# Neighbourhood scores of two heads side by side in TensorE, bias tables staged early, and an odd layer's weights loaded into the block spilled first

## The chip, the cores and the metric

The kernel runs as one program on the eight NeuronCores of one Trainium2 chip, two dies of four cores (cores 0 to 3 and 4 to 7). Each core serves 512 context tokens (two prompts) and 1024 latent tokens (one sample). The metric is the device time of the slowest core in microseconds (us).

A program on all eight cores has a slow state, in which one die runs at a lower granted TensorE clock; runs in that state are left out of every ratio. Besides it there is a milder disturbance that still counts as fast: some or all cores of one die run at a mean granted clock of about 0.98 instead of about 0.99, and the time is some 15 us longer. Beside the ratios I use a second number, the **undisturbed die**: of every run, slow ones too, each die on which no core's mean clock is below 0.986 gives the span of its slowest core, and I take the median over these dies. The cut at 0.986 is my choice.

## The reference, cut to what matters

Four layers share one residual stream y. Even layers join a short gated convolution with attention of eight heads of 64 channels; odd layers join pooling with latent attention, whose keys and values are expanded from a compressed form by `w_kv_b`. Every layer has a modulated norm and a squared-ReLU MLP.

```python
def modulate(x, g, shift, scale):
    return rms_norm(x, g) * (1 + scale) + shift

def na_latent(q, k, v, k_ctx, v_ctx, rpb):        # even layers, latent tokens, 64 columns x 16 rows
    ...                                           # keys: 8 neighbouring rows x 16 columns, and 256 cached ones
    s_loc = einsum('brcqhd,brkcjhd->bhrcqkj', qg, kb) * scale
    s_loc = s_loc + bias                          # bias = rpb[head, row offset, column offset]
    s_loc = where(valid, s_loc, NEG_INF)
    s_ctx = einsum('brcqhd,bmhd->bhrcqm', qg, k_ctx) * scale
    p = softmax(concatenate([s_loc, s_ctx], -1))
    ...

def mla_kv(ckv, kpe, w_kv_b, gk):                 # odd layers
    kv = ckv @ w_kv_b                             # the expansion
    ...
```

Of the kernel before, what the change touches and what calls it, by code (L numbers as in the profile page):

```python
# [6 lines left out]
F32 = mybir.dt.float32  # L7
BF16 = mybir.dt.bfloat16
# [83 lines left out]
class Prog:  # L92
# [103 lines left out]
    def schedule(self):  # L196
# [47 lines left out]
        while ndone < total:  # L244
            pick = None
            for e in self.ENG:
# [22 lines left out]
                if pick is None or tmin < pick[0]:  # L269
                    pick = (tmin, e, items)  # L270
            if pick is None:
                self.stuck(cand, ndone)
            tmin, e, items = pick
# [214 lines left out]
def build(depth=4):  # L488
# [43 lines left out]
    with ExitStack() as st:  # L532
# [195 lines left out]

        def SQUARE(out, in_, reads, writes, key=None):

            P.add(("act", "dve"), {"act": [act_fn(out, in_, AF.Square, None, None)],
                                   "dve": [lambda h: h.tensor_tensor(out=R(out), in0=R(in_), in1=R(in_), op=ALU.mult)]}, reads, writes,
                  {"act": act_dur(out, None, None), "dve": vdur(fsize(out))}, key=key)
# [114 lines left out]
        def norm(l, which, tb, key=None):  # L848
# [15 lines left out]
            for kc in range(8):  # L864
                tm, btm = ntr.next()
                STT(tm[:], yT[:, tb, kc, :], Asc[:, l, kc, m:m + 1], r, ALU.mult, ALU.mult,
                    [by[tb][kc], bmw, br], [btm], key=key)
# [4 lines left out]
                SHIFT(o, i_, mod[:, l, sh0 + kc, m:m + 1], ALU.add, [btm, bmw], [bh[tb][kc]], key=key)  # L872
# [109 lines left out]
        def even_bufs(tbs, ar):  # L982
# [4 lines left out]
            e.qTm, b = ar.take((128, 8, n), BF16, 8 * nb, "q")  # L987
            e.bq = {tb: [b[h * nb + k] for h in range(8)] for k, tb in enumerate(tbs)}
# [14 lines left out]
        def even_fixed(e):  # L1003

            MEMSET(e.Vx[:, :, :, 64:128], 1.0, [e.bones])
            qv = e.qTm.rearrange("p (j two) t -> p j two t", two=2)
            for tb in e.tbs:
                MEMSET(qv[64:128, :, 0, lo(tb)], 0.0, e.bq[tb])
                MEMSET(qv[0:64, :, 1, lo(tb)], 0.0, e.bq[tb])
# [30 lines left out]
        def qk_tile(l, e, which, tb, j, w, bw):  # L1040
# [11 lines left out]
            if which == 0:  # L1052
                for a in range(2):
                    ps_ = slice(a * 64, a * 64 + 64)
                    STT(e.qTm[ps_, 2 * j + a, lo(tb)], pt[ps_, :], gqna_sb[ps_, i:i + 1], r[ps_, :], ALU.mult, ALU.mult,
                        [pt.b, br, bsm], [e.bq[tb][2 * j + a]])
# [46 lines left out]
        def attT(e):  # L1103
            return e.qTm.rearrange("p (j two) t -> p two j t", two=2)[:, 0]

        def batt(e):
            return {tb: [e.bq[tb][2 * j] for j in range(4)] for tb in e.tbs}
# [9 lines left out]

        def even_att_p(l, e, key, zones):
            for j in range(4):
                P.key = key + j * 0.01  # L1120
                for a in range(2):
                    h = 2 * j + a
                    s_ = PT(P, 2, zone=zones[0])
                    MMG([(s_[:, (s * 2 + c) * 256:(s * 2 + c + 1) * 256], e.kT[:, j, s * 256 + c * 128:s * 256 + (c + 1) * 128],
                          e.qTm[:, h, s * 256:(s + 1) * 256], True, True) for s in range(2) for c in range(2)],
                        [e.bk[0][j], e.bq[0][h]], [s_.b])
                    p_, bp = e.Pr.next()
                    ACT(p_[:], s_[:], AF.Exp, [s_.b], [bp])
                    acc = PT(P, 1, zone=zones[1])
                    MMG([(acc[:, s * 256:(s + 1) * 256], vo(e, s * 2 + c, h), p_[:, (s * 2 + c) * 256:(s * 2 + c + 1) * 256], c == 0, c == 1)  # L1130
                         for s in range(2) for c in range(2)], [bp, e.bones] + e.bV[0:4], [acc.b])
                    head_out(e, h, acc, 0)

        def even_att_s(l, e, key):
            i = l // 2
            kof = lambda c, b: (c // 2) * 512 + b * 256 + (c % 2) * 128
            RG = [(0, 8, 0, 4), (0, 12, 0, 0), (4, 16, 1, 0), (8, 16, 1, 0)]
            for j in range(4):
                for a in range(2):
                    h = 2 * j + a  # L1140
                    hk = key + h * 0.1
                    P.key = hk
                    tt_, btt = e.Tt.next()
                    for u in range(4):
                        sg, bsg = e.stg.next()
                        DMA("sp", [(sg[:], rpbx[i][h * 4 + u])], [], [bsg], "stg%d" % u, key=hk - 0.3)
                        ACT(tt_[:, u // 2, (u % 2) * 480:(u % 2) * 480 + 480], sg[:], AF.Exp, [bsg], [btt[u]], key=hk - 0.1)
                    acc = [PT(P, 1, zone=[4]), PT(P, 1, zone=[5])]
                    work = [("c", 0), ("c", 1), ("r", 1), ("r", 0), ("r", 2), ("r", 3)]
                    for n, (kind, c) in enumerate(work):  # L1150
                        P.key = hk + (n - 2) * 0.01
                        s_ = PT(P, 2, zone=[0, 2])
                        sv = s_[:].rearrange("p (b x) -> p b x", b=2)
                        p_, bp = e.Pr.next()
                        if kind == "c":
                            MMG([(sv[:, b, :], e.kcT[:, j, c * 128:(c + 1) * 128], e.qTm[:, h, b * 512:512 + b * 512], True, True)
                                 for b in range(2)], [e.bkc, e.bq[1][h], e.bq[2][h]], [s_.b])
                            ACT(p_[:], s_[:], AF.Exp, [s_.b], [bp])
                            its = [(acc[b][:], vo(e, 8 + c, h), p_[:, b * 512:(b + 1) * 512], c == 0, False, True) for b in range(2)]
                            MMG(its[0:1], [bp, e.bones, e.bV[8 + c]], [acc[0].b], key=hk + n * 0.01)  # L1160
                            MMG(its[1:2], [bp, e.bones, e.bV[8 + c]], [acc[1].b], key=hk + n * 0.01)
                            continue
                        r0, r1, u, i0 = RG[c]
                        nr = r1 - r0
                        qs = e.qTm[:, h, :].rearrange("p (r x) -> p r x", x=64)
# [732 lines left out]
```

## The kernel before: the parts that the change touches

A helper records every operation; a list scheduler then puts each engine's operations in order by estimated start times and a priority `key`. Channels lie in the 128 partitions, so two heads of 64 channels share a tile. In the kernel before, q of each head was stored in its own full-height tile whose other 64 rows are zero, so that a full 128-row matmul against the keys of both heads gives one head's scores:

```python
e.qTm, b = ar.take((128, 8, n), BF16, 8 * nb, "q")
...
MEMSET(qv[64:128, :, 0, lo(tb)], 0.0, e.bq[tb])      # the other head's rows
MEMSET(qv[0:64, :, 1, lo(tb)], 0.0, e.bq[tb])
```

The bias enters as a product: exp(s + bias) = exp(s) · exp(bias). A head has four tables of 128x480 values (`rpbx`), loaded as f32 into four stage buffers `stg`, sent through an exp into `Tt`, and multiplied in:

```python
for a in range(2):                                   # one head after the other
    h = 2 * j + a
    for u in range(4):
        sg, bsg = e.stg.next()
        DMA("sp", [(sg[:], rpbx[i][h * 4 + u])], [], [bsg], "stg%d" % u, key=hk - 0.3)
        ACT(tt_[:, u // 2, (u % 2) * 480:(u % 2) * 480 + 480], sg[:], AF.Exp, [bsg], [btt[u]], key=hk - 0.1)
    ...
    MMG([(sv[:, b, 0:nr * 40]..., e.kT[:, j, kof(c, b):kof(c, b) + 128],
          qs[:, r0:r1, b * 24:b * 24 + 40], True, True) for b in range(2)], ...)   # scores, 128 rows
    ACT(pv, sv[:, :, 0:nr * 40], AF.Exp, [s_.b], [bp])
    TT(pv, pv, tv, ALU.mult, [bp] + btt[2 * u:2 * u + 2], [bp])                    # times the table
    ...                                                                          # times V, full height
```

`stg` and `Tt` share the memory of the context group's keys and values, so in layer 0 no table can be asked for before the context attention is done.

In the odd layers the second and third block of y are saved to HBM ("spilled") and their memory is used for weights. `w_kv_b` went where the block that is spilled last had been:

```python
ya, yb = spill(l, 1), spill(l, 2)
o = odd_s_bufs(ya, yb)
...
US = Slot(ya)
```

The norm was one multiply by two factors on DVE and then a shift on ACT or DVE:

```python
STT(tm[:], yT[:, tb, kc, :], Asc[:, l, kc, m:m + 1], r, ALU.mult, ALU.mult, ...)   # y * A * rstd
SHIFT(o, i_, mod[:, l, sh0 + kc, m:m + 1], ALU.add, ...)
```

The softmax here doesn't subtract the row's maximum and nothing guards it: scores larger than these inputs give would overflow.

## Time and profile before

| | before |
|---|---|
| median of 3 runs | 2410.29 us (2410.05 to 2416.41) |
| profiled run | 2394.7 us, spans of the cores 2379.0 to 2392.3 us, clocks 0.991 to 0.996 |
| TensorE (PE) busy, slowest core | 2289.2 us, 96% |

The profiled run was a quick one. The page of the slowest core starts with the engines' busy time, its share of the span and the number of instructions; its part 4 gives the engines' shares of the chain of waits that ended last:

```profile
...
PE 2289.2 (96%) x14455; PEld 1133.0 (47%) x14455; DVE 1068.7 (45%) x1668; ACT 1193.6 (50%) x1845; POOL 227.7 (10%) x377
...
PE 85%; ACT 5%; DMA 4%; DVE 3%; issue 3%; POOL 0%; DVEq 0%; ACTq 0%; POOLq 0%; SPq 0%
...
```

TensorE is the limit: nearly all of the time is its work, and the question is always where it works less or starves less. The next fence is from the groups of instructions by shape, core 0: line, engine, operation, what it reads and writes, shape, count, then busy us and mean ns of one. A busy time that sums overlapping pipelined matmuls is not the time that they take: a stream of 128x512 matmuls advances one per 0.216 us, though each lasts 0.38.

```profile
...
L644 PE MATMUL psall<-arena 128*128 128x512 bf16 x672 | 155.5, 380 | 2.3 <-DVE arena L694 1.0 <-ACT nrstd L668 0.8 <-ACT arena L668 0.5
...
L1796 PE MATMUL psall<-ones 128*128 128x128 bf16 x693 | 47.2, 229 | 0.7 <-issue 0.7
...
L644 PE MATMUL psall<-arena 128*128 128x320 bf16 x192 | 38.1, 299 | 2.4 <-ACT arena L668 1.3 <-DVE arena L679 0.7
...
L644 PE MATMUL psall<-arena 128*128 128x480 bf16 x64 | 18.2, 366 | 0.2 <-ACT arena L668 0.2
...
L644 PE MATMUL psall<-arena 128*128 128x256 bf16 x128 | 17.6, 274 | 0.0
...
```

All shapes have 128 rows: scores and products with V can't be told apart by shape, and no matmul of 64 rows exists. The 693 matmuls on `ones` are fillers that the scheduler puts into gaps to keep the clock up.

Layer 0's attention, by stretches of core 0: start and end, length, busy time of each engine, then PEclk (the granted TensorE clock), the DMA engines' busy share, and GB/s.

```profile
...
120.00:140.00 20.00, 20.00 (x97) 9.25 (x95) 10.96 (x18) 12.69 (x21) 0.02 (x1) 1.00 0.13 27
140.00:160.00 20.00, 20.00 (x160) 10.70 (x159) 11.91 (x21) 13.57 (x23) 1.57 (x3) 1.00 0.58 106
...
180.00:190.00 10.00, 9.16 (x74) 4.49 (x72) 4.77 (x10) 3.08 (x6) 1.06 (x2) 1.00 1.01 173
190.00:200.00 10.00, 10.00 (x120) 6.11 (x118) 6.92 (x12) 5.82 (x9) 1.10 (x3) 1.00 1.00 179
200.00:210.00 10.00, 5.53 (x28) 2.44 (x25) 1.18 (x2) 1.29 (x3) 0.48 (x1) 1.00 1.02 208
210.00:220.00 10.00, 6.93 (x26) 2.99 (x27) 7.19 (x11) 4.39 (x8) 0.00 (x0) 0.66 1.04 201
...
```

From 200 to 220 us TensorE works 12.5 of 20 us while DMA is full; from 120 to 140, DMA is nearly idle. The timeline of ACT in the same place (start, length, instruction; in brackets the idle time before it and what ended it) shows the exps of the tables, 128x480:

```profile
...
182.55 1.58 ACT L668 ACTIVATE arena<-arena 128x480 bf16<-128x480 f32 x3
...
189.59 0.60 ACT L668 ACTIVATE arena<-arena 128x480 bf16<-128x480 f32 x1 [2.27 <-DMA arena<-rpbx]
...
198.95 0.60 ACT L668 ACTIVATE arena<-arena 128x480 bf16<-128x480 f32 x1
...
204.22 0.60 ACT L668 ACTIVATE arena<-arena 128x480 bf16<-128x480 f32 x1 [3.71 <-DMA arena<-rpbx]
209.82 0.60 ACT L668 ACTIVATE arena<-arena 128x480 bf16<-128x480 f32 x1 [5.00 <-DMA arena<-rpbx]
...
```

They come as their loads land. The chain of waits in this place, in order of time, is one such load (start, us, what):

```profile
...
184.42 25.32 DMA arena<-rpbx
...
```

In the odd layer, all four loads of `w_kv_b` are issued late, after POOL's queue waited 6.7 us for a norm (the view of one tile, core 0):

```profile
...
L742 POOL DMA_DIRECT2D yT<-w_kv_b x4: 873/877/955, 728.1 to 730.8; - x4
...
  DVE hT L723: 6.7, 1
...
```

### The profile page before, as it was taken

How to read it: one execution, taken by the hardware profiler on the slowest of the kernel's cores; microseconds unless marked ns; L12 is line 12 of the kernel's file. 1: busy time of each engine (PE TensorE's matmuls, PEld its weight loads, DVE VectorE, ACT ScalarE, POOL GpSimd, SP SyncE). 2: the span in 40 equal slices, each digit the busy share in tenths (PEclk: the TensorE clock that was granted, in tenths of full speed). 3: DMA queues.
4: the chain of work that ended last, by engine and by line, in shares of the span. 5: the costliest groups of instructions: out<-in, count | busy, mean ns of one | idle time of the engine just before them, and what ended most of it. 6: DMA issues, size and time to landing. Idle time of an engine off the chain costs nothing.

```text
span 2392.3 us, 38889 instructions; the slowest of 8 cores (2379.0 to 2392.3 us)
## 1 busy us (share of the span) xinstructions
PE 2289.2 (96%) x14455; PEld 1133.0 (47%) x14455; DVE 1068.7 (45%) x1668; ACT 1193.6 (50%) x1845; POOL 227.7 (10%) x377
## 2 busy tenths in 40 slices
PE   5998999999999999999999999999999999899999
PEld 4454444444444555444444444444445445444444
DVE  2555654324546643323444666531454674243222
ACT  2763636133546675622643775515334657662233
POOL 3100000010001300000002001000100120000000
PEclk9999999999999999999999999999999999999999
DMA  9759686579365778523666666765955635322342
GB/s 184 148 85 177 164 149 129 106 135 153 76 169 78 137 162 142 102 45 83 127 145 146 133 151 131 146 124 114 158 106 133 115 78 120 69 53 53 73 86 88
DMA packets 75286, 285.61 MB, mean 119 GB/s; under 512 B 28896, under 2 KB 41952, under 8 KB 47328
## 3 DMA queue, kind: packets, MB, share of 16 engines
q0 software_dynamic: 52240, 205.27, 50.5%
q1 hardware_dynamic: 22864, 77.87, 9.6%
q8 instruction: 119, 1.95, 0.3%
q14 instruction: 63, 0.52, 0.1%
HBM read 456.23 MB, written 30.54 MB: 203 GB/s over the span
## 4 chain that ended last, share of the span: by engine, by line
PE 85%; ACT 5%; DMA 4%; DVE 3%; issue 3%; POOL 0%; DVEq 0%; ACTq 0%; POOLq 0%; SPq 0%
PE psall L644 84%; ACT arena L668 3%; DMA arena<-rpbx 2%; DVE arena L679 1%; DMA WT<-ada_w 1%; PE psall L652 1%; DVE arena L694 1%; DVE ntmp L694 1%; DMA arena<-mlp_w 1%; PE psall L1796 1%; DMA WT<-mlp_w 0%; ACT psall L668 0%; ACT hT L668 0%; DMA yT<-even_conv 0%; POOL rtmp L679 0%
## 5 line engine op out<-in xcount | busy, mean ns | idle before, releaser
L694 DVE SCALAR_TENSOR_TENSOR yT<-psall,mod,yT 128x512 f32<-128x512 f32 x480 | 358.9, 750 | 680.5 <-PE psall L644 679.9
L644 PE MATMUL psall<-arena,WT 128*128 128x512 bf16 x2688 | 594.9, 379 | 2.6 <-DVE rtmp L679 1.4
L644 PE MATMUL psall<-hT,arena 128*128 128x512 bf16 x2472 | 551.3, 379 | 2.6 <-DVE hT L716 1.5
L668 ACT ACTIVATE arena<-psall 128x512 bf16<-128x512 f32 (+6 forms) x629 | 408.7, 660 | 215.1 <-PE psall L644 171.9
L644 PEld LDWEIGHTS psall<-arena,WT 128*128 128x128 bf16 x2688 | 260.4, 98 | 310.3 <-issue 4.0
L668 ACT ACTIVATE psall<-psall 128x512 f32<-128x512 f32 (+1 forms) x330 | 191.7, 581 | 413.8 <-PE psall L644 412.7
L644 PE MATMUL psall<-arena 128*128 128x65 bf16 (+9 forms) x2960 | 368.1, 273 | 22.9 <-ACT arena L668 15.1
L644 PEld LDWEIGHTS psall<-hT,arena 128*128 128x128 bf16 x2472 | 240.2, 98 | 287.8 <-issue 3.4
L644 PE MATMUL psall<-hT,WT 128*128 128x512 bf16 x1504 | 345.3, 381 | 8.8 <-ACT hT L668 3.5
L644 PEld LDWEIGHTS psall<-arena 128*128 128x128 bf16 (+1 forms) x2960 | 196.6, 97 | 185.0 <-issue 42.7
L668 ACT ACTIVATE nsq<-yT 128x1024 bf16<-128x1024 f32 x66 | 69.6, 1055 | 338.7 <-PE psall L644 211.9
L644 PEld LDWEIGHTS psall<-hT,WT 128*128 128x128 bf16 x1504 | 144.9, 98 | 179.2 <-issue 19.4
L668 ACT ACTIVATE arena<-psall,rk 128x1024 bf16<-128x1024 f32 (+1 forms) x224 | 196.6, 933 | 60.7 <-PE psall L644 56.2
L644 PE MATMUL psall<-hT,yT 128*128 128x512 bf16 x704 | 166.1, 381 | 11.9 <-ACT arena L668 10.3
L694 DVE SCALAR_TENSOR_TENSOR ntmp<-yT,A,nrstd 128x512 f32<-128x512 f32 x192 | 136.3, 750 | 45.4 <-ACT nrstd L668 41.0
L668 ACT ACTIVATE hT<-ntmp,mod 128x512 bf16<-128x512 f32 x161 | 111.3, 719 | 29.0 <-DVE ntmp L694 28.1
L644 PEld LDWEIGHTS psall<-hT,yT 128*128 128x128 bf16 x704 | 68.5, 98 | 92.5 <-issue 15.9
L694 DVE SCALAR_TENSOR_TENSOR arena<-psall,cst_sb,rstd 64x512 bf16<-64x512 f32 (+2 forms) x102 | 76.2, 748 | 75.4 <-ACT rstd L668 72.9
L742 POOL DMA_DIRECT2D WT<-mlp_w x56 | 30.3, 542 | 611.0 <-PE psall L644 608.0
L644 PE MATMUL psall<-arena,yT 128*128 128x512 bf16 (+3 forms) x480 | 77.5, 304 | 1.6 <-ACT arena L668 0.8
L679 DVE TENSOR_TENSOR mod<-psall,cst_sb 128x8 f32<-128x8 f32 x48 | 7.9, 165 | 157.5 <-PE psall L644 157.0
L668 ACT ACTIVATE psall<-psall,eps_sb 128x512 f32<-128x512 f32 x84 | 55.3, 658 | 33.3 <-PE psall L644 33.1
(111 smaller groups left out, 1466.3 us busy)
## 6 DMA issues: line engine op xcount, KB each, us to landing
WT<-mlp_w POOLq DMA_DIRECT2D x56, 1024.0 KB, 9.9
arena<-ada_w POOLq DMA_DIRECT2D x38, 1024.0 KB, 11.2
arena<-mlp_w POOLq DMA_DIRECT2D x32, 1024.0 KB, 9.8
ysc<-yT SPq DMA_DIRECT2D x9, 2048.0 KB, 8.0
yT<-ysc SPq DMA_DIRECT2D x18, 1024.0 KB, 13.2
arena<-rpbx SPq DMA_DIRECT2D x64, 240.0 KB, 7.6
yT<-even_conv POOLq DMA_DIRECT2D x12, 768.0 KB, 9.6
WT<-ada_w POOLq DMA_DIRECT2D x8, 1024.0 KB, 10.8
```

Of the source, the lines that this page charges most:

```text
L644: h.matmul(R(out), lhsT=lhsT, rhs=rhs, start=start, stop=stop, skip_group_check=skip))
L652: fns = [lambda h, o=o, a=a: h.transpose(R(o), a, ident[:, :]) for (o, a) in items]
L668: return lambda h: h.activation(out=R(out), in_=R(in_), func=func, **kw)
L679: fn = [lambda h: h.tensor_tensor(out=R(out), in0=R(in0), in1=R(in1), op=op)]
L694: P.add("dve", [lambda h: h.scalar_tensor_tensor(out=R(out), in0=R(in0), scalar=scalar, in1=R(in1), op0=op0, op1=op1)], reads, writes, vdu ...
L742: fns = [lambda h, o=o, i_=i_: h.dma_start(out=o, in_=i_) for (o, i_) in pairs]
L1796: P.warm = lambda h, o: h.matmul(o, lhsT=ones[:, :], rhs=ones[:, :], start=True, stop=True)
```

## The change

Its intent, in the order of expected worth:

1. q of two heads in one tile (half the memory, no zeros). Scores of the two heads as two 64-row matmuls that can run at once in the upper and lower half of TensorE. Attention goes by pairs of heads and half images.
2. The smaller q leaves room for the four stage buffers elsewhere, so that the first four tables are asked for earlier. The next pair's tables go through the same four buffers.
3. `w_kv_b` and the weights of the query expansion (`w_q_b`) go into the block of y that is spilled first; the pooling projection's weights and output, which had been there, go into the other one. And the first block's projections go ahead of the cache's expansion.
4. The norm becomes a plain multiply, on DVE or POOL, whichever the scheduler finds free, and a scale-and-shift on ACT or DVE. The scheduler breaks ties by priority.

The core of the diff, with cuts marked:

```diff
-            e.qTm, b = ar.take((128, 8, n), BF16, 8 * nb, "q")
+            e.qT, b = ar.take((128, 4, n), BF16, 4 * nb, "q")
...
+        def scores(tile, pairs, reads, key=None):
+            for (out, lhsT, rhs) in pairs:
+                for a in range(2):
+                    r = slice(a * 64, a * 64 + 64)
+                    fns.append(lambda h, o=out(a), l=lhsT(r), x=rhs(r): h.matmul(R(o), lhsT=l, rhs=x, start=True, stop=True))
...
             for j in range(4):
+                t2, btt = e.Tt.next()
                 for a in range(2):
                     for u in range(4):
                         sg, bsg = e.stg.next()
-                        DMA("sp", [(sg[:], rpbx[i][h * 4 + u])], [], [bsg], "stg%d" % u, key=hk - 0.3)
+                        DMA("sp", [(sg[:], rpbx[i][(2 * j + a) * 4 + u])], list(after), [bsg], "stg%d" % u, key=hk - 0.3)
...
-            e.stg = ring(ar, (128, 480), F32, 4, "stg")
+            e.stg = ring(Arena(e.stg_off), (128, 480), F32, 4, "stg")
...
-                STT(tm[:], yT[:, tb, kc, :], Asc[:, l, kc, m:m + 1], r, ALU.mult, ALU.mult, ...)
+                TT(tm[:], yT[:, tb, kc, :], r, ALU.mult, [by[tb][kc], br], [btm], eng="any", key=key)
...
-                SHIFT(o, i_, mod[:, l, sh0 + kc, m:m + 1], ALU.add, ...)
+                SCALE(o, i_, Asc[:, l, kc, m:m + 1], mod[:, l, sh0 + kc, m:m + 1], ...)
...
-            o = odd_s_bufs(ya, yb)
+            o = odd_s_bufs(yb, ya)
...
-            US = Slot(ya)
+            US = Slot(yb)
-            P.key = T + 4
-            kv_block(l, o, "c", ck, bck)
             for tb in (1, 2):
                 odd_prod(l, o, tb, T + 1 + (tb - 1) * 4)
+                if tb == 1:
+                    P.key = T + 4
+                    kv_block(l, o, "c", ck, bck)
```

## The prediction

> **What bounds the kernel.** The page shows PE busy 2289 of 2392 us (96%); the chain of waits is 84% PE matmuls, with pieces of ACT (3%) and of loads of `rpbx` (2%). A stream of 128x512 matmuls advances one per 0.216 us (eight in 1.89 us, the last being 0.38 long). Time is thus PE work plus places where PE starves: about 103 us idle and about 39 us of warm-up matmuls on `ones` (693, each about 0.056 us).
>
> **Scores by two heads.** Per even layer, scores stream 64 heads-by-keys matmuls of about 512 to 256 columns. Summed over both even layers from the groups by shape (64x512, 64x320, 64x480 and 64x256 columns at 0.42 ns each): about 42 us. As two 64-row halves side by side, ideally 21 us. The Trainium skill, "TensorEngine Tiling (Array Packing)", Key Properties, says that changing the tiling mode drains TensorE. No 64-row matmul exists in the trace before, so I cannot measure that. There are 64 score groups per even layer, nearly all between full-height matmuls, so about 256 mode changes. A matmul's latency beyond its stream time is 0.16 us (0.38 - 0.22), an upper estimate of a drain; then 41 us would be lost, twice the gain. I take about 0.05 us: 13 us back. Net 8 us saved, possibly 20, possibly a small loss. AV matmuls and exp elements stay equal; exps per pair of heads go from 12 to 14 (about 0.2 us each, ACT is 70 to 80% busy there, not limiting).
>
> **Layer 0 tables.** The timeline shows p attention holding the buffers for bias tables until 174 us; `rpbx` loads then start behind saturated DMA, ACT waits 7.0 and 6.6 us, and PE sits idle 10.3 us at 189 to 199 (busy 8.9 of 20). Half-size q frees room, so four loads come early. I expect 8 to 10 us saved, some given back because total bytes stay the same and DMA is about 75% busy until 340 us. The second table wait (269 us, PE about 4 us idle) may stay.
>
> **Odd layers.** `w_kv_b` is loaded at 735 us, only after the norm of the third block freed its y (POOL waits 6.9 us for hT); from 721 to 736 PE has only norm sums, warm-up matmuls (about 70) and 4 us idle. With the weights in the block spilled first they can be issued about 13 us earlier, so key/value and query expansion fill this gap and the latency-bound stretch at 785 to 812. Same at 1866 to 1882. Worth 3 to 5 us per odd layer, 8 in all.
>
> **Rest.** Zeroing of q goes (12.5 us POOL at start, but start is DMA-bound: weights arrive until 41 us, 1.0 of DMA busy): 0 to 2 us. One 128-row STT replaces two 64-row ones (0.76 us each, x48): DVE time, mostly hidden. The norm's multiply may go to POOL; its chain stays limited by two buffers (0.83 us a tile): about 0, perhaps lock trouble between DVE and POOL.
>
> **Sum.** 8 + 9 + 8 + 3 = about 28 us: 2410 to 2382 us, range 2358 to 2405. Faster by over 2%: 0.15; within: 0.82; slower: 0.03.
>
> **Shows it.** Score matmuls in pairs start nearly together, with PE time by shape halved; gaps at the change between 64-row and 128-row matmuls give the drain; PE busy in 180 to 200 near 20; `w_kv_b` issued near 722 and fewer matmuls on `ones`; layer 2's attention (1340 to 1480, PE 99%) shortens by the tiling's net gain alone.
>
> **Wrong if** the drain is 0.15 us per change (tiling loses 20 us), if it is near 0 (then 2370), if DMA takes back layer 0's gain, or if reordering by the list scheduler (its tie rule changes too) opens new gaps.

## The result and the profile after

The changed kernel took 2414.37 us (median of 4 runs, 2413.57 to 2414.81) against 2410.68 for the kernel before (4 runs, with the three above): ratio 1.001, 95% interval 0.9992 to 1.0027, that is, the same within 2%. A ratio is the mean time of one kernel's fast runs over that of the other's of the same rounds, so it is not quite the ratio of the medians quoted. Five of the eight dies in those four runs were mildly disturbed. On undisturbed dies of later runs (r1 and g3 below) the changed kernel takes 2397.6 us (15 dies) against 2389.6 (57 dies): it is about 8 us slower. 2414.37 us is outside the predicted range of 2358 to 2405 us. That 2397.6 lies inside it is no success: the range was counted from 2410, and 28 us less than 2389.6 would be about 2362.

The same lines of the page after, here of core 5, which is on a disturbed die:

```profile
...
PE 2300.6 (95%) x14344; PEld 1106.1 (46%) x14344; DVE 1087.6 (45%) x1705; ACT 1147.5 (48%) x1777; POOL 270.4 (11%) x404
...
PE 84%; ACT 4%; DVE 4%; DMA 4%; issue 3%; POOL 1%; ACTq 0%; DVEq 0%; SPq 0%; POOLq 0%
...
```

All views below are of core 0, whose die ran at 0.989. The groups by shape:

```profile
...
L1816 PE MATMUL psall<-ones 128*128 128x128 bf16 x518 | 38.1, 236 | 4.3 <-DVE arena L717 2.2 <-DVE arena L680 1.2 <-issue 0.9
...
L1123 PE MATMUL psall<-arena 64*128 64x320 bf16 x128 | 19.3, 309 | 0.3 <-ACT arena L669 0.2
...
L1123 PE MATMUL psall<-arena 64*128 64x512 bf16 x64 | 11.8, 391 | 0.5 <-ACT arena L669 0.5
...
L1123 PE MATMUL psall<-arena 64*128 64x256 bf16 x64 | 5.8, 273 | 0.0
L1123 PE MATMUL psall<-arena 64*128 64x160 bf16 x64 | 5.0, 233 | 1.7 <-ACT arena L669 1.7
...
```

There are now 320 matmuls with 64 rows (line L1123), and only 518 fillers on `ones`. How two of them run shows in the timeline of TensorE:

```profile
...
123.88 0.39 PE L1123 MATMUL psall<-arena 64*128 64x256 bf16 x4
124.20 1.90 PE L645 MATMUL psall<-hT,yT 128*128 128x512 bf16 x7
...
```

Four 64-row matmuls of 256 columns take 0.39 us from the start of the first to the end of the last. In the single records the two halves of a pair start 3 ns apart, which agrees with the Trainium skill, "TensorE: Matmul & The Clock Gate", Part 3, Measured speedup vs the span model: about 4 ns per tile. So the two halves do run side by side. But the same records give the price. A core changes 208 times between 128-row and 64-row matmuls, and at each change the next matmul starts later than the columns of the one before explain: by 96 ns (median) on the way into 64-row mode and by 102 ns on the way out, on every core alike. Other changes from one group of matmuls to the next have a median of 0. That is 208 × 0.099 = 20.6 us per core. The Trainium skill, "TensorEngine Tiling (Array Packing)", Key Properties, says that a change of mode drains TensorE; this is the size of that drain here.

Layer 0's attention after the change, in the same stretches:

```profile
...
120.00:140.00 20.00, 19.89 (x97) 8.72 (x97) 8.62 (x14) 12.73 (x21) 0.53 (x1) 1.00 0.44 88
140.00:160.00 20.00, 18.96 (x125) 8.88 (x125) 8.94 (x17) 13.54 (x23) 1.06 (x2) 1.00 0.58 107
...
180.00:190.00 10.00, 8.13 (x66) 4.13 (x68) 6.98 (x13) 2.68 (x5) 1.06 (x2) 1.00 1.03 162
190.00:200.00 10.00, 8.21 (x40) 3.41 (x39) 3.86 (x6) 1.20 (x2) 0.53 (x1) 1.00 1.01 174
200.00:210.00 10.00, 3.26 (x9) 1.31 (x10) 3.08 (x5) 0.60 (x1) 0.00 (x0) 0.66 1.00 219
210.00:220.00 10.00, 8.06 (x47) 3.20 (x46) 3.76 (x7) 8.14 (x13) 0.53 (x1) 0.83 0.73 162
...
```

The hole in DMA at 120 to 140 us is half filled (0.44 instead of 0.13), by the early tables. Yet from 180 to 220 us TensorE works 27.7 us instead of 31.6, and its clock is below 1 in two stretches instead of one. The Trainium skill, "TensorE: Matmul & The Clock Gate", Part 1, describes just that: after an idle window of about 3.4 us TensorE falls to half clock until it has been busy again; 0.66 in a stretch of 10 us is about two such windows. The trace agrees: TensorE was idle from 199.9 to 206.7 us, and the clock was 0.50 from 203.0 to 209.8. The exps of the tables tell why:

```profile
...
184.11 2.08 ACT L669 ACTIVATE arena<-arena 128x480 bf16<-128x480 f32 x4 [6.34 <-DVE arena L680]
...
198.12 0.60 ACT L669 ACTIVATE arena<-arena 128x480 bf16<-128x480 f32 x1 [4.24 <-DMA arena<-rpbx]
205.40 0.60 ACT L669 ACTIVATE arena<-arena 128x480 bf16<-128x480 f32 x1 [6.67 <-DMA arena<-rpbx]
210.15 1.20 ACT L669 ACTIVATE arena<-arena 128x480 bf16<-128x480 f32 x2 [4.15 <-DMA arena<-rpbx]
...
```

Four tables were staged early, but their place in `Tt` still came free only at 184 us. Then the other four of the pair were asked for, in the middle of a full DMA, and landed by 198, 205 and 210 us. The chain of waits in this window, in order of time, is a single load (start, us, what):

```profile
...
185.79 24.27 DMA arena<-rpbx
...
210.15 0.55 ACT arena L669
...
212.68 0.37 PE psall L1123
```

The kernel before had such a load in the same place, from 184.42 to 209.74 us. So the load lands within 0.4 us of the same time; what differs is how much work TensorE can do before it lands: 24.7 of the 30 us from 180 to 210 before, 19.6 after.

In the odd layer `w_kv_b` is issued 5 us later on the clock, but layer 0 ends 18.2 us later on this core (718.8 instead of 700.6 us), so that relative to it the loads come 13.1 us earlier:

```profile
...
L749 POOL DMA_DIRECT2D yT<-w_kv_b x4: 873/877/892, 733.2 to 735.9; - x4
...
  DVE yT L695: 4.5, 1
...
```

And the norm, first before and then after (count, then min/median/max ns of one):

```profile
...
L723 DVE TENSOR_SCALAR hT<-ntmp,mod x31: 479/486/568, 79.3 to 2115.5; 128x512 bf16<-128x512 f32 x31
...
```

```profile
...
L732 DVE TENSOR_SCALAR hT<-ntmp,A,mod x109: 530/546/1630, 44.0 to 2123.0; 128x512 bf16<-128x512 f32 x109
...
L680 POOL TENSOR_TENSOR ntmp<-yT,nrstd x47: 1260/1442/1816, 40.1 to 2121.1; 128x512 f32<-128x512 f32 x47
...
```

POOL takes 47 of the 192 multiplies of the norm at 1.44 us each. Of DVE's 109 scale-and-shifts, the 45 that overlap a multiply of POOL have a median of 1.17 us (up to 1.61), the other 64 one of 0.54 (one of these, beside a memset of POOL, took 1.63). That is in line with the exclusive lock on the port that DVE and GpSimd (POOL) share in the Trainium skill, "SBUF — State Buffer", SBUF: two separate sides.

To see where time went I split the matmul records of each core's profiled run at four instructions (DVE adds into y 480 times; the 24th, 120th, 240th, 360th and last of these end the parts) and put every interval from one matmul's start to the next under one of five heads: **work** (its columns, at 0.216 us for 512, and at least some 0.03 us an instruction), fillers, **drain** (up to 0.1 us at a change of mode), **clock** (time lost at a granted clock below 1), and **idle** (what is left is gaps below 0.1 us, 2 to 5 us in all). Means over the eight cores in us; "after" is its run g3, in which no die was disturbed:

| part | | total | work | fillers | drain | clock | idle |
|---|---|---|---|---|---|---|---|
| start to the first block's end of layer 0 | before | 347.0 | 259.1 | 24.8 | 0 | 8.8 | 52.0 |
| | after | 360.0 | 250.5 | 22.4 | 10.0 | 14.4 | 60.1 |
| rest of layer 0 (MLP) | before | 356.2 | 348.0 | 0 | 0 | 0.6 | 7.4 |
| | after | 356.5 | 346.3 | 0 | 0 | 1.0 | 9.2 |
| layer 1 | before | 589.8 | 553.2 | 7.5 | 0 | 2.0 | 26.6 |
| | after | 583.6 | 551.3 | 2.7 | 1.1 | 4.5 | 23.2 |
| layer 2 | before | 555.2 | 544.0 | 0.9 | 0 | 0 | 10.2 |
| | after | 559.4 | 535.4 | 0 | 8.9 | 0.4 | 13.9 |
| layer 3 | before | 533.0 | 491.5 | 5.5 | 0 | 2.3 | 32.1 |
| | after | 526.7 | 491.4 | 3.7 | 0 | 5.2 | 24.3 |
| whole | before | 2381.1 | 2196.8 | 38.7 | 0 | 13.7 | 128.2 |
| | after | 2386.2 | 2175.9 | 28.9 | 20.1 | 25.5 | 130.5 |

Work fell by 20.9 us, as predicted (21). The drains took 20.1 of them back. The two odd layers won 6.2 and 6.3. Layer 0's first part lost 13.0, and layer 2 lost 4.2. One caution for what follows: some variants do a few us of the MLP's work ahead of the first cut or behind it. Where the work of the first part differs by more than 2 us I therefore give layer 0 as a whole (703.2 us before, 716.5 after).

### The profile page after: what moved, and what is told of

Same layout as the page of the kernel before. It is cut to its first block, busy times and chain, and to the rows that moved or that the text cites. A ratio compares the mean times of both kernels' runs of the same rounds, so it can differ in the third digit from the quotient of the medians.

```text
span 2412.8 us, 38773 instructions; the slowest of 8 cores (2386.0 to 2412.8 us)
## 1 busy us (share of the span) xinstructions
PE 2300.6 (95%) x14344; PEld 1106.1 (46%) x14344; DVE 1087.6 (45%) x1705; ACT 1147.5 (48%) x1777; POOL 270.4 (11%) x404
## 4 chain that ended last, share of the span: by engine, by line
PE 84%; ACT 4%; DVE 4%; DMA 4%; issue 3%; POOL 1%; ACTq 0%; DVEq 0%; SPq 0%; POOLq 0%
PE psall L645 82%; ACT arena L669 2%; DMA arena<-rpbx 2%; PE psall L1123 1%; DMA WT<-ada_w 1%; DVE arena L680 1%; PE psall L653 1%; POOL ntmp L680 1%; DVE hT L732 1%; PE psall L1816 1%; DMA arena<-ada_w 1%; DVE arena L695 1%; ACT psall L669 0%; DVE ntmp L680 0%; POOL rtmp L680 0%
## 5 line engine op out<-in xcount | busy, mean ns | idle before, releaser
L695 DVE SCALAR_TENSOR_TENSOR yT<-psall,mod,yT 128x512 f32<-128x512 f32 x480 | 359.0, 750 | 717.3 <-PE psall L645 716.9
L645 PE MATMUL psall<-hT,arena 128*128 128x512 bf16 x2472 | 558.9, 382 | 2.8 <-DVE hT L717 2.8
L669 ACT ACTIVATE arena<-psall 128x512 bf16<-128x512 f32 (+5 forms) x645 | 410.9, 647 | 261.6 <-PE psall L645 162.0
L645 PE MATMUL psall<-arena 128*128 128x65 bf16 (+6 forms) x2704 | 325.7, 267 | 30.7 <-DVE arena L680 20.0
L645 PEld LDWEIGHTS psall<-arena 128*128 128x128 bf16 (+1 forms) x2704 | 171.7, 97 | 180.4 <-issue 47.4
L680 DVE TENSOR_TENSOR ntmp<-yT,nrstd 128x512 f32<-128x512 f32 x145 | 102.3, 737 | 40.7 <-ACT nrstd L669 40.3
L645 PEld LDWEIGHTS psall<-hT,yT 128*128 128x128 bf16 x704 | 66.1, 98 | 87.2 <-issue 14.4
L680 POOL TENSOR_TENSOR ntmp<-yT,nrstd 128x512 f32<-128x512 f32 x47 | 70.6, 1503 | 202.7 <-ACT nrstd L669 164.0
L695 DVE SCALAR_TENSOR_TENSOR arena<-psall,cst_sb,rstd 128x512 bf16<-128x512 f32 (+1 forms) x78 | 58.1, 746 | 74.9 <-ACT rstd L669 73.9
L669 ACT ACTIVATE hT<-ntmp,mod,A 128x512 bf16<-128x512 f32 x83 | 64.9, 809 | 47.2 <-DVE ntmp L680 38.4
L732 DVE TENSOR_SCALAR hT<-ntmp,A,mod 128x512 bf16<-128x512 f32 x109 | 84.4, 792 | 5.3 <-POOL ntmp L680 1.2
## 6 DMA issues: line engine op xcount, KB each, us to landing
arena<-ada_w POOLq DMA_DIRECT2D x38, 1024.0 KB, 11.9
```

Source lines behind the costliest of these rows:

```text
L645: h.matmul(R(out), lhsT=lhsT, rhs=rhs, start=start, stop=stop, skip_group_check=skip))
L669: return lambda h: h.activation(out=R(out), in_=R(in_), func=func, **kw)
L680: fn = [lambda h: h.tensor_tensor(out=R(out), in0=R(in0), in1=R(in1), op=op)]
L695: P.add("dve", [lambda h: h.scalar_tensor_tensor(out=R(out), in0=R(in0), scalar=scalar, in1=R(in1), op0=op0, op1=op1)], reads, writes, vdu ...
L732: fv = lambda h: h.tensor_scalar(out=out, in0=in_, scalar1=s, scalar2=v, op0=ALU.mult, op1=ALU.add)
```

## The experiments

Theories at the start: **T1**, a change of mode costs 0.1 us and eats the tiling's gain; **T2**, layer 0 loses because a pair of heads needs eight tables where a head needed four, and only four are staged; **T3**, the rewritten norm (POOL's multiplies, the lock) costs DVE time that the critical path sees; **T4**, the odd layers' order is a gain by itself. Rivals stand with the runs. All runs are compared by the undisturbed die (before 2389.6, after 2397.6), with the ratio to the kernel before, and by the parts of the table above.

| run | what | undisturbed die, us (dies) | ratio to before, 95% |
|---|---|---|---|
| r1, g3 | changed kernel again, twice | 2397.5 (7), 2397.6 (8) | 0.9999 [0.9953, 1.0045], 0.9963 [0.9944, 0.9983] |
| e1 | after, scores full height | 2398.6 (8) | 1.0039 [1.0025, 1.0053] |
| e2 | after, old norm | 2388.7 (6) | 1.0003 [0.9987, 1.0019] |
| e3 | after, old tie rule | 2395.0 (9) | 1.0031 [1.0015, 1.0047] |
| e4 | after, old odd layers | 2414.2 (6) | 1.0108 [1.0089, 1.0127] |
| e5, g4 | before, new odd layers, twice | 2384.1 (5), 2377.6 (4) | 0.9974 [0.9921, 1.0027], 0.9906 [0.9846, 0.9967] |
| e6 | after, norm's multiply on DVE | 2396.1 (8) | 1.0018 [1.0002, 1.0034] |
| e7 | after, old norm, tables in order of use | 2383.1 (8) | 0.9936 [0.9881, 0.9991] |
| e8 | after, score groups by two | 2396.6 (8) | 0.9997 [0.9951, 1.0044] |
| h1 | after, half the tables | 2387.7 (8) | 0.9998 [0.9974, 1.0022] |
| h2 | before, half the tables | 2391.6 (8) | 1.0001 [0.9979, 1.0023] |
| h3 | after, old norm, eight stages | 2375.9 (8) | 0.9934 [0.9919, 0.9950] |
| g1 | after, eight stages | 2377.5 (7) | 0.9881 [0.9859, 0.9903] |
| k1 | after, other queue, four stages | 2396.2 (8) | 1.0012 [0.9983, 1.0041] |
| g2, k2 | h3 and score groups by two, twice | 2369.3 (6), 2368.9 (10) | 0.9882 [0.9794, 0.9969], 0.9904 [0.9882, 0.9927] |

The ratios differ between chips where the runs of the kernel before fell on mildly disturbed dies: in the group with g1 to g4 all four of its fast runs did, in that with r1, e5, e7 and e8 three of six. So those two groups' ratios flatter the variants, and the third column decides.

### e1: what is the tiling worth?

Wrong on purpose (relative error 0.032): each head's scores take all 128 rows, so both heads get the sum. Same schedule, no 64-row matmul.

```diff
-                    r = slice(a * 64, a * 64 + 64)
+                    r = slice(0, 128)
```

> Changed kernel, but each score matmul takes all 128 rows of both heads (wrong result on purpose; same instructions, same order on every engine). Theory: the trace shows 104 score groups bounded by 208 mode changes, 96 ns in and 102 ns out, 20.6 us in all, and streaming halved from about 42 to 21 us, so both cancel: 2411 to 2418 us against 2414. Rival (the tiling gain is real and was lost elsewhere, in norms or order): full height is about 20 us slower, 2430 to 2436 us.

Measured: 2398.6 us against 2397.6. By the parts, work goes back up to 2196.6 us (+20.7 us) and drains fall from 20.1 to 0. The tiling as it stands is worth about nothing: 1 us by the undisturbed die, and 1.5 us the other way by the sum of the parts (2384.7 without it, 2386.2 with it). Layer 0's first part hardly moved either, 359.0 against 360.0 us, so its loss isn't the tiling's.

### e2, e3, e4: one part of the change undone at a time

```diff
 e2: the norm as before
-                TT(tm[:], yT[:, tb, kc, :], r, ALU.mult, [by[tb][kc], br], [btm], eng="any", key=key)
+                STT(tm[:], yT[:, tb, kc, :], Asc[:, l, kc, m:m + 1], r, ALU.mult, ALU.mult, ...)
-                SCALE(o, i_, Asc[:, l, kc, m:m + 1], mod[:, l, sh0 + kc, m:m + 1], ...)
+                SHIFT(o, i_, mod[:, l, sh0 + kc, m:m + 1], ALU.add, ...)
 e3: the scheduler's tie rule as before
-                if pick is None or (tmin, top) < (pick[0], pick[3]):
+                if pick is None or tmin < pick[0]:
 e4: the odd layers' blocks and order as before
-            o = odd_s_bufs(yb, ya)
+            o = odd_s_bufs(ya, yb)
...
```

> Changed kernel with the norm of before (one DVE multiply by A and r, then shift). Theory: the new norm sends 47 multiplies to POOL (1.5 us each), which hold up DVE (35 us of DVE time in the trace) and let PE wait and its clock fall to half; undoing it gives 8 to 15 us: 2399 to 2406 us. Rival (the loss in layer 0 is the tables or the order alone): within 3 us of 2414.

Measured: 2388.7 us, 9 us less than the changed kernel, within the 8 to 15 expected; by the sum of the parts, a mean over the cores, only 4.7 less (2381.5). The gain is spread: layer 2 556.1 us (3.3 less), layer 3 2.4 less, layer 0's first part 360.8 (none).

> Changed kernel with the tie rule of the list scheduler as before. Theory: the rule moves only order, within 4 us of 2414. Rival (the new order opened the gaps of layer 0): 8 us or more faster, 2406 or less.

Measured: 2395.0 us, 2.6 less than the changed kernel: layer 0's first part 356.4 (3.6 less), but with 3.4 us of work moved behind the cut, so that layer 0 as a whole is only 0.8 shorter; layer 2 561.1 (1.7 more). The sum of the parts is 0.7 more. A small matter, near what one reshuffling of the schedule does.

> Changed kernel with the odd layers' expansion weights in the block spilled second, as before. Theory: the swap is worth the 5 to 6 us per odd layer by which the two traces' odd layers differ, so undoing it costs 8 to 12 us: 2422 to 2427 us. Rival (odd layers gained by other parts, such as the norm): within 3 us of 2414.

Measured: 2414.2 us, 16.6 more than the changed kernel, where 8 to 12 were expected. Layers 1 and 3 went from 583.6 and 526.7 to 593.5 and 534.6 us, 17.8 together: about 12 more of idle and 7.7 of fillers, and some 2 less lost to the clock. The loads of `w_kv_b` moved as the prediction said, here in the view of one tile of e4:

```profile
...
L749 POOL DMA_DIRECT2D yT<-w_kv_b x4: 873/880/963, 746.3 to 749.0; - x4
...
```

746.3 us against 733.2 in the changed kernel, although e4's layer 0 ended 3.0 us sooner on this core. T4 stands, for the place of the weights and the order of the expansion together: no run moved one without the other.

### r1 and g3: the changed kernel as the reference

> The changed kernel again, unedited, beside the kernel before on this job's chip, as the reference for the variants. Theory (the change is a real zero to small loss: 21 us saved on score streaming, 20 us of mode changes, 13 us lost in layer 0, 12 to 17 us won in the odd layers): ratio to before 1.001 to 1.005. Rival (the small loss was only the lower granted clock of that chip's second die): ratio 0.993 to 0.998 on a chip without those stretches.

> The changed kernel unedited, as reference for the other three on one chip: ratio to before 0.999 to 1.005 on an undisturbed chip.

Measured: ratios 0.9999 and 0.9963, on a chip where the kernel before was often mildly disturbed (three of its six and four of its four fast runs) and the changed kernel only once by my cut (one die of r1; in the trace of that run no core has a clock record of 13/16, so its 0.985 comes from half-clock stretches alone). The undisturbed dies say 2397.5 and 2397.6, 8 us above the kernel before, as three undisturbed dies of its first four runs do (2397.7). So r1's ratio fits neither theory's reading of a ratio, and g3's is below its range; it was the denominator that moved. This is why the second metric was needed.

### e5 and g4: the odd layers alone

The kernel before with e4's hunk in the direction of the change.

> The kernel before with nothing but the reordering of the odd layers (weights in the block spilled first, the cache's expansion after the first block's products). Theory: undoing it alone cost 8 to 9 us per odd layer, so alone it should win 14 to 18 us: ratio 0.992 to 0.994, faster than both kernels. Rival (the odd layers gain only in the new kernel, where layer 0 and 2 end later): ratio 0.997 to 1.000.

> The kernel before with the reordering of the odd layers alone, again on another chip: if both dies are undisturbed, ratio to before 0.991 to 0.995; the two odd layers together shorter by 13 to 18 us. If it is 0.997 or above with both dies at the same clock, the reordering gains less by itself than it does in the changed kernel.

Measured: 2384.1 and 2377.6 us, 5 and 12 below the kernel before, with few undisturbed dies (5 and 4), as these runs often fell on disturbed ones. The parts are steadier: layer 1 586.6 and 585.9 (before 589.8), layer 3 525.3 and 525.0 (before 533.0), so 10.9 and 11.9 us together, less than the 14 to 18 expected of e5 and the 13 to 18 expected of g4. e5's ratio of 0.9974 is in its rival's range, but three of its four runs and three of the six of the kernel before had a disturbed die. On undisturbed dies the reordering alone beats both kernels; what it wins by itself, 11 to 12 us, is less than what undoing it costs the changed kernel, 17.8. In both directions layer 3 moves by about 8 us, and the difference lies in layer 1.

### e7: the tables in order of use

The changed kernel with the old norm; the first four stage buffers take the two tables of each head that are used first.

```diff
-                for a in range(2):
-                    for u in range(4):
+                for side in range(2):
+                    for a, u in ((0, side * 2), (0, side * 2 + 1), (1, side * 2), (1, side * 2 + 1)):
```

> The changed kernel with the norm as before and the eight table loads of a pair of heads in the order of use: first both heads' tables of the first two kept chunks (first four stage buffers), then the others. Theory (layer 0's loss is the wait of a pair of heads for eight tables, of which only four are staged): the 7 to 10 us gap at 199 to 212 us shrinks below 3 us and the segment from start to the end of layer 0's attention loses 7 to 9 us: ratio to the changed kernel 0.996. Rival (DMA is full there, so the wait moves to the next use): same segment within 2 us of the changed kernel's.

Measured: 2383.1 us, 5.6 less than with the old norm alone (e2). But layer 0's first part is 358.9 against 360.8, 1.9 us less instead of 7 to 9, and the gap, instead of shrinking, grew into one of 15.7 us (core 0, up to 211 us): TensorE got further and then waited for the other four. That is what the rival said: order doesn't help, since the loads that are missing are in a full DMA. The remaining gain (layer 2, 2.4 us less, layer 0's MLP 2.1 less, and small amounts elsewhere) I can't assign.

### h1 and h2: half the tables

Both use the first head's tables for the second head too, in layer 0 only (the bias is small enough that the result still passed the tolerance). Their outputs are wrong, which doesn't matter for the times. Half of layer 0's table loads are gone.

```diff
+                        if a == 0 or l:
-                        DMA("sp", [(sg[:], rpbx[i][(2 * j + a) * 4 + u])], ...
+                            DMA("sp", [(sg[:], rpbx[i][(2 * j + a) * 4 + u])], ...
```

> The changed kernel, wrong on purpose: in layer 0 the second head of each pair uses the first head's four tables, so half of the table loads are gone (16 instead of 32) and nothing else. Theory (a pair of heads needs eight tables before its attention can run, and the last four come through a full DMA): the idle of TensorE at 195 to 212 us, 7 to 10 us in the changed kernel, falls under 3 us, and the time from start to the end of layer 0's attention and projection of the first block (360 to 362 us) falls by 8 us or more. Rival (the tables' wait stands for a general backlog of weight loads behind them): the gap stays over 5 us and the segment falls by less than 4 us.

> The kernel before with the same edit (layer 0's odd heads use the even heads' tables; wrong on purpose). Theory: it waits for four tables at a time, so it gains less than the changed kernel does: the same segment (347 us) falls by 2 to 5 us. If it falls by as much as in the changed kernel, the grouping by pairs isn't what costs the difference.

Measured: the changed kernel gains 9.9 us (2387.7), its first part falls from 360.0 to 354.0, and on no core is there a gap over 2.1 us left at 195 to 212 us. The fall of 6.0 is short of the 8 expected, but above the rival's 4. The kernel before gains nothing: 2391.6 us, where I had expected 2 to 5 us less in the first part. That part is 351.3 instead of 347.0, with 5.0 us of work moved ahead of the cut, so that layer 0 as a whole is the same, 702.9 against 703.2. Its largest gap around 195 to 212 us is still 6 to 12 us on seven of the eight cores, and on core 0 the chain there is still one load of `rpbx`, 25.5 us long, that lands at 210.4. So halving the table bytes does nothing for the kernel before and much for the changed one: what costs is the eight tables that a pair needs at once. T2 stands, with a part of the loss open.

### h3, g1 and k1: eight stage buffers

h3 and g1 load the tables as bf16 into eight stage buffers in the same memory. The load then converts, and is issued on POOL's queue, as this kernel's converting weight loads already are. h3 has the old norm as well, g1 the new one. k1 makes the change of queue and type alone and keeps four buffers.

```diff
-                        DMA("sp", [(sg[:], rpbx[i][(2 * j + a) * 4 + u])], list(after), [bsg], "stg%d" % u, key=hk - 0.3)
+                        DMA("pool", [(sg[:], rpbx[i][(2 * j + a) * 4 + u])], list(after), [bsg], "stg%d" % (a * 4 + u), key=hk - 0.3)
-            e.stg = ring(Arena(e.stg_off), (128, 480), F32, 4, "stg")
+            e.stg = ring(Arena(e.stg_off), (128, 480), BF16, 8, "stg")
```

> The changed kernel with the norm as before and the tables' stage buffers as eight of bf16 instead of four of f32 (the load converts, on the POOL queue), so that all eight tables of the first pair are asked for at about 117 us, where DMA is only 0.4 busy. Correct. Theory: the gap at 195 to 212 us falls under 3 us, the segment to 350 to 353 us, ratio to before on an undisturbed chip 0.990 to 0.993. Rival (general backlog of loads): the gap stays above 5 us. It may also lose by POOL's queue issuing the tables in line with the weights.

> The changed kernel with eight bf16 stage buffers, its own norm kept. Theory (the wait for eight tables is most of layer 0's loss, the norm's rewrite costs 3 to 5 us in layer 2 and 1 to 3 us in layer 0): the segment to the end of layer 0's attention at 348 to 352 us, layer 2 at 559 to 562, ratio to before 0.995 to 0.998. Rival (the norm makes most of layer 0's loss): the segment stays over 357 us.

> The changed kernel with the table loads converted to bf16 on the POOL queue, but still four stage buffers. Theory (the number of stages is the cause): the segment to the end of layer 0's attention stays at 357 us or more and the gap of TensorE at 195 to 212 us over 5 us; slowest core of an undisturbed die near 2397 us. Rival (the software queue serves the tables sooner): the segment falls to 348 to 353 us and the core to 2380.

Measured: g1, which differs from the changed kernel in this alone, takes 2377.5 us, 20.1 less; its first part falls from 360.0 to 349.8 (idle 52.7 instead of 60.1, clock 8.7 instead of 14.4), its layer 2, which loads tables in the same way, from 559.4 to 555.3 (559 to 562 was expected; with the old norm the stages do not shorten it, 557.2 in h3 against 556.1 in e2), and the sum of the parts by 16.4. h3 takes 2375.9, first part 346.7. The result is correct in both. But the gap that closed is not won against the kernel before: these first parts, 349.8 and 346.7 us, stand against its 347.0, and idle in them is 52.7 and 48.9 us against 52.0. In g1 the eight exps run in one row, and no wait for a load stands before them (timeline of ACT, core 0):

```profile
...
183.44 4.05 ACT L669 ACTIVATE arena<-arena 128x480 bf16<-128x480 bf16 x8 [6.33 <-DVE arena L680]
...
```

```profile
...
120.00:140.00 20.00, 20.00 (x99) 8.74 (x97) 8.46 (x14) 12.27 (x20) 4.24 (x8) 1.00 0.73 101
...
180.00:190.00 10.00, 9.70 (x78) 4.62 (x79) 8.00 (x17) 5.93 (x11) 5.40 (x11) 1.00 1.02 146
190.00:200.00 10.00, 9.53 (x54) 4.03 (x51) 4.33 (x8) 8.53 (x14) 2.12 (x4) 1.00 1.06 156
200.00:210.00 10.00, 8.32 (x76) 3.99 (x77) 6.90 (x14) 7.21 (x13) 2.27 (x5) 1.00 1.07 167
210.00:220.00 10.00, 10.00 (x58) 3.99 (x55) 5.33 (x10) 6.14 (x10) 1.15 (x3) 1.00 1.05 157
...
```

The early hole in DMA is used (0.73 at 120 to 140 us), TensorE works 37.6 us of 180 to 220 instead of 27.7, and the clock stays at 1.00.

k1 comes out at 2396.2 us with a first part of 359.3: the time of the changed kernel. So for the whole time it is the number of stages, not the queue. In layer 0 the queue has some part in it: k1 does 3.4 us of work more ahead of the cut, and as a whole its layer 0 is 712.1 us against 716.5 (g3) and 704.4 (g1); layer 1 then takes 3.9 more. One thing I expected of k1 failed: no gap over 5 us is left at 195 to 212 us. The other queue spreads the same waiting over more and shorter ones (idle 57.1 in the part against 60.1 in g3 and 52.7 in g1). The size of the largest gap is a poor measure of a wait; the part's total is a good one.

g1 against h3 also prices the norm once more: 1.6 us on the undisturbed die, and 0.7 in the sum of the parts (2369.8 and 2369.1). The 9 us of e2 show only while the tables are late. So T3, as a cost of its own, is not shown; how the norm and the late tables act together is open.

### e6: the norm's multiply on DVE

```diff
-                TT(tm[:], yT[:, tb, kc, :], r, ALU.mult, [by[tb][kc], br], [btm], eng="any", key=key)
+                TT(tm[:], yT[:, tb, kc, :], r, ALU.mult, [by[tb][kc], br], [btm], key=key)
```

> The changed kernel with the norm's multiply held on DVE instead of on whichever of DVE and POOL is free; its scale-and-shift stays free to go to ACT or DVE. Theory (POOL's 47 multiplies of 1.5 us slow DVE's instructions that run beside them by some 35 us in all, and the chain of the norm waits for them): about the same as with the old norm, that is 4 to 8 us less than the changed kernel (ratio to before near that of the old norm's, 0.997 to 1.001), with layer 2 at 554 to 557 us instead of 559 to 562. Rival (the two-instruction form itself is worse, wherever it runs): layer 2 stays at 559 or above.

Measured: 2396.1 us, 1.5 less than the changed kernel, where 4 to 8 were expected. Layer 2 did fall to 556.9, but layer 0's first part rose to 367.1. So POOL's multiplies lengthen single DVE instructions beside them, as the trace shows, but taking them away doesn't give the time back: with respect to the total, this reading of T3 falls.

### e8, g2 and k2: half as many changes of mode

The scores of two groups go out together into four PSUM banks. e8 is the changed kernel with that, g2 and k2 are h3 with that.

```diff
-                    s_ = PT(P, 2, zone=zones[0])
-                    scores(s_, [... for c in range(2)], ...)
+                s_ = PT(P, 4, zone=None if zones[0] is None else [0])
+                scores(s_, [... for s in range(2) for c in range(2)], ...)
... and likewise for the latent tokens
```

> The changed kernel with the score groups issued two at a time into four PSUM banks, so that TensorE changes between 128-row and 64-row mode about half as often. Theory (each change costs about 0.1 us, 208 of them): about 105 changes, drain total 10 instead of 20 us, 6 to 10 us faster if nothing else opens: ratio to the changed kernel 0.996 to 0.9975. Rival (the exps of a pair must end before the four banks are free, so PE waits for ACT): PE idle in attention of layer 2 rises by over 8 us and the time is the same or longer.

> The version with eight bf16 stages and the norm as before, its score groups issued two at a time (four PSUM banks). Theory (fewer mode changes, but the four banks come free later): changes fall from 210 to about 145, drains from 20 to 14 us, while idle of TensorE rises by 5 to 8 us: ratio to the version without grouping 0.999 to 1.001. Rival (with the tables there in time the drains saved show): idle rises by less than 2 us and the ratio is 0.997 to 0.998.

> The best version again (eight bf16 stages, norm as before, scores two groups at a time). If its size is real: slowest core of an undisturbed die 2368 to 2372 us, ratio to before 0.990 to 0.993 where neither has a disturbed die in its fast runs.

Measured: changes fall to 144, not to the 105 that I expected of e8: seven score groups make four pairs, not three and a half, and in the changed kernel some groups already stood side by side (208 changes for 128 groups). A change again costs 96 ns in and 92 out, and drains are 13.6 us instead of 20.1, so the price per change holds. In e8 this gives 1.0 us (by the sum of the parts it is 4.0 longer), and idle and fillers rise by about 7 us each. That is the rival's sum, but not its place: idle in layer 2 fell by 1.7 us instead of rising by over 8; it rose in layer 0's first part (63.9 against 60.1) and in the odd layers. On top of h3 it gives 6.6 to 7.0 us (2369.3 and 2368.9 against 2375.9), about the drains saved; idle rises by only 2.2 to 2.5 us and fillers by 2.1, while the clock loses 5.5 to 6 us less, so that the match with the drains is in part chance. The same saving of TensorE time was thus worth nothing in e8 and about its full size on h3. A likely reason is that layer 0 waits in e8 for a load that lands at a fixed time (on core 0 its chain is one load of `rpbx` that lands at 210.29 us, against 210.07 in the changed kernel). This isn't shown: e8 and h3 differ in the norm as well as in the stages, and e8 loses time in layers 1 and 3 too (2.6 and 0.9 us). g2's theory, that idle takes the saving back, falls. This version is correct and beats both kernels: k2's four fast runs took 2371.91 to 2376.79 us, ratio 0.9904, interval 0.9882 to 0.9927, and 20.7 us less than the kernel before on undisturbed dies.

## Why the prediction was wrong

The prediction was 28 us less, 2382 us. The result is 2414.37 us, and on undisturbed dies about 8 us more than before. Step by step:

- **What bounds the kernel: right.** TensorE's work plus the places where it starves accounts for the time in both kernels.
- **"As two 64-row halves side by side, ideally 21 us": right.** Work fell by 20.9 us, and e1 gave 20.7 back.
- **"I take about 0.05 us: 13 us back": the mechanism was right, the size wrong.** The term was mis-sized on both factors: a change costs 0.099 us, and there are 208 changes, not 256. Together 20.1 us come back instead of 13, so the tiling nets about 1 us or less instead of 8. The list of what would make the prediction wrong had it, at 0.15 us.
- **"Layer 0 tables ... 8 to 10 us saved": this is the step that failed.** I saw that half-size q lets four loads come early, and missed that the change also made a pair of heads the unit, which needs eight tables before its attention can run where a head needed four. Four early tables for a unit of eight leave four to be asked for from 184 us on, when the place for their exps comes free, in a full DMA (1.00 to 1.03 busy). They landed up to 210 us. The first part lost 13.0 us: idle 8.1, and clock 5.6 for the pauses, against a prediction of 8 to 10 saved. h1 (half the loads) wins 6.0 of it back, g1 (eight stages) 10.2, and h3 (eight stages and the old norm) all of it. The prediction had named "DMA takes back layer 0's gain", but not the doubled need. Its premise, that the wait of the kernel before was worth 8 to 10 us, is not borne out by any run: with all eight tables in time (g1, h3) the first part takes 349.8 and 346.7 us against its 347.0, and idle in it is 3 us less at best (48.9 in h3 against 52.0). (h2 is no test of this: with half the loads the last one still lands at 210.4 us.) So closing the gap undid the loss and won next to nothing beyond it; what TensorE waits for instead stays open.
- **"Odd layers ... 8 in all": right, somewhat low.** 12.5 us were won from before to after, 11 to 12 by the reordering alone (e5, g4), and 17.8 are lost without it (e4). The loads of `w_kv_b` come 13.1 us earlier relative to the end of layer 0; predicted were about 13.
- **"Rest", 0 to 2 us for the zeroing and about 0 for the norm: not resolved.** Undoing the norm gave 9 us (e2) in the schedule of the change, and 1.6 (g1 against h3) once the tables were in time. POOL's multiplies lengthen single DVE instructions, and that is not seen in the total (e6). That the zeroing went was never tested alone.
- **"Layer 2's attention shortens by the tiling's net gain alone": wrong.** There, work fell by 8.6 us, drains cost 8.9, and 3.7 us of idle came on top: layer 2 is 4.2 longer. With eight stages it is 555.3 (g1), with the old norm 556.1 (e2), and with both 557.2 (h3); its small waits are spread over many places, and I did not settle what makes them.

The sum of the parts: +13.0 and +0.3 in layer 0, -6.2 in layer 1, +4.2 in layer 2, -6.3 in layer 3, +5.0 us on the mean of the cores (+5.1 before rounding). Of the 36 us between prediction and undisturbed die, about 22 are layer 0's first part (9 predicted, 13.0 lost, of which g1 puts 10.2 down to the stages), about 7 the drain's size, and the rest lies in layer 2 and in what the slowest core adds to the mean, less what the odd layers won beyond the 8.

## What to carry to other kernels

Packing two half-height matmuls side by side pays only by what a stretch of them saves beyond two changes of mode, here 0.2 us. A score group here saved 0.16 us on average (20.9 us over 128 groups), so single groups are not worth it; put several together before changing back. When a change makes the unit of work larger (a pair of heads instead of a head), count again everything that must be there before a unit can start, its loads and its buffers, and stage a whole unit. And measure a stage by its total rather than by its largest gap: eight stages closed a gap that in the kernel before, too, is 7 to 11 us long on seven of eight cores, and the first part became at most 0.3 us shorter than that kernel's.

## What the Trainium skill lacked or had wrong

- "TensorEngine Tiling (Array Packing)", Key Properties, says that a change of mode drains TensorE but gives no time. Here it is 96 ns into and 92 to 102 ns out of 64-row mode, 20 us per core for 208 changes. Its list When to Use Tiling recommends row tiling for a contraction of 64 or less without that cost; here 64-row tiling of 64-channel heads saved 20.9 us of work and cost 20.1 in drains.
- "TensorE: Matmul & The Clock Gate", Part 1, advises to budget 13/16 of the clock for dense matmuls on all cores. Here eight cores with TensorE busy 95 to 96% of the time ran at mean clocks of 0.986 (my cut) to 0.998 on undisturbed dies; only the slow state came near 13/16 as a mean (0.812 to 0.839 on the slow die of the five longest runs, 2756 to 2805 us). That the clock can fall to 13/16 for a spell alone I found on no page: in the traces with the mild disturbance it is 60 to 162 us of some 2400.
- "SBUF — State Buffer", SBUF: two separate sides, describes the lock between DVE and GpSimd. The runs agree that DVE instructions beside POOL's multiplies get longer (scale-and-shifts have a median of 1.17 us there and of 0.54 elsewhere). It doesn't say what such waits cost a whole kernel; here removing the multiplies took only 1.5 us off the total.
